# Where five groups of small operations stand in the queues of a projection-bound decoder layer

## The chip, the cores and the metric

The kernel runs on one core of a Trainium2 chip. A core has five engines, each with its own queue that it works through in order: TensorE (PE; its weight loads are listed apart as PEld), VectorE (DVE), ScalarE (ACT), GpSimd (POOL) and SyncE (SP). SP, ACT and POOL also issue DMA transfers from their queues. The time of a kernel is the device time of one execution in microseconds (us); of several runs the median is given.

## The reference

One layer with a residual: a norm, one input projection, three token mixers on separate groups of heads (gated DeltaNet with 6 heads, gated linear attention "GLA" with 5, forgetting attention "fox" with 5), their gates, one output projection, and a final norm. 512 tokens and 16 meta tokens, width 2048, all in float32.

```
h = rms_norm(concat(meta, x), norm_w);  proj = pad(h) @ w_in
qkv = silu(conv4(dq, dk, dv));  q, k = l2_normalize(...)
# gated DeltaNet, chunks of 64, g = cumsum(log_a) in the chunk
decay = exp(where(causal, g[:, None] - g[None, :], -inf))
a_mat = where(strict, (k*beta) @ k.T * decay, 0)
u, w  = triangular_solve(eye + a_mat, [v*beta, k*beta*exp(g)])
# over chunks: v_new = u - w @ s; o = (q*exp(g)) @ s + qk @ v_new; s = s*exp(g_last) + k_dec.T @ v_new
# GLA: chunked linear attention with a decay per key dimension; fox: softmax with cumulative log gates
y = x + concat(dn, gla, fox) @ w_out
return rms_norm(y, final_norm_w)[:, 16:]
```

## The kernel before

**Weights in halves.** The work is bound by two large projections. Float32 precision is kept by splitting each operand in two parts: a high one (rounded to the multiplying type) and a low one (what is left). A "half" is a weight tile `raw` of 128 x 1024 (512 KB), loaded on SP's queue. `split` turns it into `whi` on ACT (line 170) and `wlo` on DVE (line 171); both are recorded with a high priority, and all `wlo` of the program are kept in the list `splits`, all `whi` in `heads_`. PE then makes three products of each 128 x 128 block, high with high, high with low, low with high, so `wlo` is used from the third multiplication of a half on. In the input projection (line 245) a half is 48 multiplications of 264 columns. In the products of the output projection (line 1399, `whia`, `wloa`, `whis`, `wlos`, and at the end `wlh`, `wll`) five pairs of blocks make a product of 60 multiplications of 512 columns.

**Who sets the order.** A scheduler orders the recorded operations on each engine by priority and its own estimate of times. A dependency of kind NoSync between two operations of one engine sets only their order there; one of kind Sync also makes an engine wait for the other. The list `waits` (read at line 1333) takes an operation and a number, and puts the operation behind the split of that number on its engine. `paced` puts an operation behind the newest split on its engine.

**The five places.**

- *Gates and decays.* `gates()` (from line 452) computes the cumulated log decays of 17 heads (6 betas, 6 decays, 5 fox gates in one tile `ga` of 17 rows) on DVE, stores them to DRAM (`gd`, line 467, on ACT's queue), and transposes them to `gcol`. `dn_keys(g)`, for groups g = 0 and 1 of three DeltaNet heads each, loads its rows of `gd` broadcast to all partitions (`gb`, line 657), transposes the keys on PE (`pk`, line 680), and makes the decays: DVE subtracts and clips (line 687: `atm` for the meta tokens, 3 of 16 x 16, and `at`, 12 of 128 x 128), ACT exponentiates (line 688).
- *The inverse.* For each group, the 51 rows of `ab` (48 blocks of 32 x 32, 3 of meta tokens) are inverted row by row on DVE, stored to DRAM (`sc`, line 751), and read back in another layout (`iv`, line 754, and `xm`, line 756), all three on ACT's queue. DVE transposes them (line 760), and PE multiplies on (`pm`, line 766).
- *Sums of x.* For Strassen-like products of the input projection, `x_sums` makes sums of x for eight k, in three calls (0 to 2, 3 to 5, 6 and 7). For each k POOL issues two loads into row buffers (`xa`, `xb`, lines 533 and 534), ACT scales one part (line 537), then come three times a sum on DVE (line 540), its high part `t` on ACT (line 541) and its low part on DVE (line 542).
- *Products of the output projection.* There are seven; behind each, `take` adds the four PSUM banks (`pq`, `pr`, `ps`) to the running outputs `acc`, `accs` on DVE (line 1418).
- *Final weights.* `weigh` multiplies twelve output tiles by the final norm's weights on POOL (line 1428), after their squares have been taken on ACT (line 1425). The last blocks' weights are split at the same time (`wlh`, `wll`).

Of the kernel before, what the change touches and what calls it, by code (L numbers as in the profile page):

```python
# [27 lines left out]
H = 3  # L28
NN = NB * H
# [53 lines left out]
def tile_hybrid_trunk(ctx, tc, xT, xtok, mtok, w_gate, w_in, w_out, w_dn, consts, lmask, fin_w, out, dbg=None):  # L83
# [372 lines left out]
    def gates():  # L456
# [9 lines left out]
        V.tensor_tensor_scan(ga[gr], scm[gr], gt[gr], 0.0, ALU.mult, ALU.add)  # L466
        nc.scalar.dma_start(out=gd, in_=ga[gr])
        pt = psm.tile([P, 512], F32, tag="m", name="ptg")
# [52 lines left out]

    xt_ = {}

    def x_sums(ks):
# [5 lines left out]
        for k in ks:  # L530
            o3 = three[k]
            r1, r2 = row(f"xa{k}")[:, :T], row(f"xb{k}")[:, :T]
            nc.gpsimd.dma_start(out=r1, in_=xT[:, k])
            nc.gpsimd.dma_start(out=r2, in_=xT[:, k + 8])
            x11, x12, x21, x22 = r1[:, :HT], r1[:, HT:], r2[:, :HT], r2[:, HT:]
            w1, w2 = nwc[:, k : k + 1], nwc[:, k + 8 : k + 9]
            A.activation(x11, x11, AF.Copy, scale=w1)
            for i, (n, x, w, less) in enumerate((("t1", x12, w1, x11), ("t2", x22, w2, x12), ("t4", x21, w2, x22))):
                hi, lo = xt_[n, k] = o3[:, i, :HT], o3[:, i, HT:]
                V.scalar_tensor_tensor(out=x, in0=x, scalar=w, in1=less, op0=ALU.mult, op1=ALU.subtract)  # L540
                A.activation(hi, x, AF.Copy, scale=-1.0)
                V.scalar_tensor_tensor(out=lo, in0=x, scalar=-1.0, in1=hi.bitcast(F32), op0=ALU.mult,
                                       op1=ALU.subtract)
# [105 lines left out]
    def dn_keys(g):  # L649
# [25 lines left out]
        for b in (4, 0, 1, 2, 3):  # L675
# [9 lines left out]
            with tc.issue_after(inverse[g - 1]) if g else ExitStack():  # L685
                for j in range(H):
                    V.tensor_scalar(e[:r, j, :], gb[:r, j, ts], gcl(b, j), 0.0, ALU.subtract, ALU.min)
            A.activation(e, e, AF.Exp)
# [37 lines left out]
    def dn_inverse(g, st):  # L726
# [17 lines left out]
        for j in range(1, 31):  # L744
# [4 lines left out]
            V.tensor_tensor(out=a3[:, j + 1 :, 0:j], in0=a3[:, j + 1 :, 0:j], in1=t3, op=ALU.add)  # L749
        sc2 = drp.tile([NN * 4 + H, 1024], F32, tag="sc2", name=f"sc2{g}", bufs=2)  # L750
        nc.scalar.dma_start(out=sc2, in_=ab)
        iv = six.tile([P, 4, NN, 32], F32, tag="six", name=f"iv{g}")
        xc, uc, m1, l1 = (iv[:, i] for i in range(4))
        nc.scalar.dma_start(out=xc, in_=sc2[0 : NN * 4].rearrange("(n r) (a c) -> (r a) n c", r=4, a=32))
        xm = t15(f"xm{g}", (32, H, 32))
        nc.scalar.dma_start(out=xm, in_=sc2[NN * 4 : NN * 4 + H].rearrange("h (a c) -> a h c", a=32))
        um = t15(f"um{g}", (32, H, 32))
# [669 lines left out]
    def weigh(tb, cc):  # L1427
        G.tensor_tensor(out=acc[tb, cc], in0=acc[tb, cc], in1=fw[cc], op=ALU.mult)  # L1428

# [75 lines left out]
    def product(p_, n, weights, first, last):  # L1505
        for j in pairs:
            w = halves(load_s(weights(j), f"{n}{j}"))
            for k in range(4):
                tb, c = k // 2, k % 2
                mms(p_[k], ops[n, j], w[c], slice(tb * P, (tb + 1) * P), first and j == 0, last and j == pairs[-1])  # L1510

    def take(p_, h, J):
        for k in range(4):
            add(2 * h + k // 2, 2 * J + k % 2, p_[k], op=ALU.subtract if J else ALU.add)

# [17 lines left out]
    product(pa, "a22", lambda j: tw[j, 3], False, True)  # L1533
    take(pa, 1, 0)


    fw = []
    for c in range(4):
# [3 lines left out]
    for cc in range(4):  # L1542
# [3 lines left out]
        for kp in kps:  # L1546
            run(pa, cc, kp, kp == kps[0], kp == kps[-1])
            if cc < 3 and (3 == 3 or cc == 2 and kp >= NP // 2 - 3):
                load_last(kp if cc == 2 and 3 < 3 else NP // 2 - 3 + cc)
        if cc == 3:  # L1550
            break
# [3 lines left out]
    for cc in range(3):  # L1555
        for tb in range(4):
            weigh(tb, cc)
    if LAST:
# [97 lines left out]
```

## Time and profile before

| what | us |
|---|---|
| median of three runs | 996.36 |
| lowest, highest | 995.36, 996.70 |
| the profiled execution's own time | 997.14 |
| its span, first to last instruction | 995.4 |
| PE busy | 978.2 |
| DVE busy | 673.5 |
| ACT busy | 480.5 |
| POOL busy | 221.6 |
| mean granted clock of PE | 0.995 |

The trace comes from the profiled execution, so its sums are compared with 997.14 and its span of 995.4. A row of a group or a timeline names the source line, the operation, and what it writes and reads; a bracket gives the idle time of the engine before it and what ended that. A row of the chain gives start and length of a piece of the chain of work that ended last.

### The profile page before, as it was taken

Reading aid. Unit: us, or ns where it says so; the run is one execution under the profiler, and the core shown is the slowest. Engines: PE = TensorE matmul, PEld = TensorE weight load, DVE = VectorE, ACT = ScalarE, POOL = GpSimd, SP = SyncE. Lnnn points to the kernel's source line nnn. Section 1 sums busy time; section 2 is a strip of 40 time slices with the busy share of each in tenths; the row PEclk is TensorE's granted clock in tenths of the full one; section 3 lists DMA queues with packets and bytes.
Section 4 is the critical chain, followed back from the end, with each engine's and each line's share of the span. In section 5 each row is a group of like instructions: output and inputs, shape, how many; then the busy total and the mean of one; then the engine's idle time right before and its main releaser. Section 6 shows DMA issues by size and latency. Waiting matters only on the chain.

```text
span 995.4 us, 19833 instructions
## 1 busy us (share of the span) xinstructions
PE 978.2 (98%) x7762; PEld 895.4 (90%) x7762; DVE 673.5 (68%) x1462; ACT 480.5 (48%) x1051; POOL 221.6 (22%) x237
## 2 busy tenths in 40 slices
PE   9998999999999999999999999999999999999996
PEld 7898999898999988899998988899999998878875
DVE  5456786866666995434684856867768768986674
ACT  7653533324546343424645535655555545644345
POOL 0021222232122334201212221323322120000042
PEclk9999999999999999999999999999999999999998
DMA  9835578977656886645644656678766578356534
GB/s 347 305 107 175 178 220 222 244 216 229 180 164 191 234 237 168 181 105 127 172 117 136 164 142 198 186 215 227 201 198 161 186 268 290 129 208 212 187 111 170
DMA packets 70291, 191.82 MB, mean 193 GB/s; under 512 B 14030, under 2 KB 17278, under 8 KB 69429
## 3 DMA queue, kind: packets, MB, share of 16 engines
q1 hardware_dynamic: 46048, 152.53, 43.9%
q0 software_dynamic: 15104, 31.66, 18.0%
q10 hardware_dynamic: 9044, 6.36, 2.3%
q8 instruction: 61, 1.00, 0.4%
q14 instruction: 34, 0.27, 0.1%
HBM read 179.84 MB, written 60.88 MB: 242 GB/s over the span
## 4 chain that ended last, share of the span: by engine, by line
PE 84%; DVE 7%; DMA 4%; issue 2%; ACT 1%; POOL 1%; ACTq 0%; DVEq 0%; POOLq 0%
PE pp L245 39%; PE pp_a L574 8%; PE pp L314 5%; PE pq L1399 4%; PE pa L1399 3%; PE ps L1399 3%; PE pt L1399 2%; PE pp_b L574 2%; PE pp_d L574 2%; PE pp_c L574 2%; PE pss L1048 1%; DVE wlo L171 1%; PE pgate L431 1%; PE pr L1399 1%; PE pfa L1226 1%
## 5 line engine op out<-in xcount | busy, mean ns | idle before, releaser
L245 PE MATMUL pp<-xh,wlo 128*128 128x264 f32 (+2 forms) x1120 | 274.1, 306 | 3.7 <-DVE wlo L171 3.7
L245 PE MATMUL pp<-xh,whi 128*128 128x264 f32 (+2 forms) x1120 | 273.5, 306 | 0.4 <-ACT whi L170 0.4
L245 PE MATMUL pp<-xl,whi 128*128 128x264 f32 (+2 forms) x1120 | 273.9, 307 | 0.0
L170 ACT CAST whi<-raw 128x1024 fp32r<-128x1024 f32 x131 | 137.2, 1048 | 182.5 <-PE pp L245 94.6
L171 DVE TENSOR_TENSOR wlo<-raw,whi 128x1024 fp32r<-128x1024 f32 x131 | 163.2, 1245 | 69.4 <-ACT whi L170 60.2
L245 PEld LDWEIGHTS pp<-xh,wlo 128*128 128x128 f32 x1120 | 183.6, 189 | 12.9 <-DVE wlo L171 4.4
L245 PEld LDWEIGHTS pp<-xh,whi 128*128 128x128 f32 x1120 | 182.9, 189 | 10.0 <-ACT whi L170 0.6
L245 PEld LDWEIGHTS pp<-xl,whi 128*128 128x128 f32 x1120 | 183.2, 189 | 9.0 <-issue 0.4
L390 POOL TENSOR_SCALAR stc<-cv 128x528 f32<-128x528 f32 (+1 forms) x18 | 28.1, 1563 | 151.0 <-DVE cv L616 148.3
L616 DVE SCALAR_TENSOR_TENSOR cv<-pb,cpk,cv 128x528 f32<-128x528 f32 (+1 forms) x54 | 41.1, 761 | 0.8
L1428 POOL TENSOR_TENSOR acc<-acc,fw 128x512 f32<-128x512 f32 x4 | 6.4, 1619 | 135.7 <-ACT sqf L1425 135.7
L171 DVE TENSOR_TENSOR wlos<-raws,whis 128x1024 fp32r<-128x1024 f32 x20 | 24.1, 1224 | 13.7 <-ACT whis L170 13.6
L170 ACT CAST whis<-raws 128x1024 fp32r<-128x1024 f32 x20 | 20.6, 1050 | 26.0 <-PE pq L1399 11.2
L574 PE MATMUL pp_a<-t,whi 128*128 128x264 f32 (+1 forms) x224 | 30.3, 283 | 0.0
L574 PEld LDWEIGHTS pp_a<-t,whi 128*128 128x128 f32 x224 | 28.0, 188 | 0.4
L574 PE MATMUL pp_a<-xh,whi 128*128 128x264 f32 x112 | 28.1, 285 | 0.0
L574 PE MATMUL pp_a<-xl,whi 128*128 128x264 f32 x112 | 27.9, 285 | 0.0
L1399 PE MATMUL pq<-whia,a 128*128 128x512 f32 x80 | 25.4, 393 | 0.0
L1399 PE MATMUL ps<-whis,s 128*128 128x512 f32 x80 | 25.3, 394 | 0.0
L1399 PE MATMUL pq<-whis,s 128*128 128x512 f32 x80 | 25.3, 394 | 0.0
L390 POOL TENSOR_SCALAR stdz<-zdz 128x512 f32<-128x512 f32 x6 | 11.2, 1876 | 63.1 <-DVE zdz L408 62.1
L493 POOL DMA_DIRECT2D tw<-tw x16 | 13.3, 834 | 45.8 <-DVE wlo L171 31.6
(506 smaller groups left out, 2118.4 us busy)
## 6 DMA issues: line engine op xcount, KB each, us to landing
raw<-in_w_in SPq DMA_DIRECT2D x103, 512.0 KB, 3.8
ti<-in_w_in SPq DMA_DIRECT2D x28, 512.0 KB, 5.4
raw<-ti SPq DMA_DIRECT2D x28, 512.0 KB, 4.0
tw<-in_w_dn SPq DMA_DIRECT2D x20, 512.0 KB, 5.2
raws<-tw SPq DMA_DIRECT2D x15, 512.0 KB, 3.3
ti<-in_w_in POOLq DMA_DIRECT2D x14, 512.0 KB, 5.8
ti<-ti POOLq DMA_DIRECT2D x14, 512.0 KB, 6.3
tw<-in_w_dn POOLq DMA_DIRECT2D x10, 512.0 KB, 6.8
```

Of the source, the lines that this page charges most:

```text
L170: pace[0] = A.copy(hi, raw).ins
L171: pace[1] = V.tensor_tensor(out=lo, in0=raw, in1=hi.bitcast(F32), op=ALU.subtract).ins
L245: mm = PE.matmul(p_[:, :nt], wt[:, j * m : (j + 1) * m], xx[k][:, t0 : t0 + nt], start=(k == 0 and wt is hi and xx is xh), stop=(k == KT - ...
L314: mm = PE.matmul(ps[:, :S], wt[:, j * P : (j + 1) * P], xx[k][:, NM:T], start=(k == 0 and wt is hi and xx is xh), stop=(k == KT - 1 and wt ...
L390: maxes.append(G.tensor_scalar_max(t, src, LOW).ins)
L431: PE.matmul(pgate[a][:, :HT], wg[k // 8][:, k % 8, :], xx[k][:, a * HT : (a + 1) * HT], start=(k == 0 and xx is xh), stop=(k == KT - 1 and ...
L493: x = G.dma_start(out=out_[s], in_=in_[s], accum_op=ALU.add, max_dma_last_dim=2048)
L574: m = PE.matmul(p_[:, cols], wt[:, j * P : (j + 1) * P], xx[j][part_][:, cols], start=first and i == 0, stop=i == len(todo) - 1, skip_grou ...
L616: V.scalar_tensor_tensor(out=c, in0=pb[:, t0 + w : w + T], scalar=cwc[:, blk, w : w + 1], in1=c, op0=ALU.mult, op1=ALU.add)
L1048: mm = PE.matmul(ps[o0 : o0 + n, b * n : b * n + n], kx[rr, k0 : k0 + n], qx[rr, q0 : q0 + n], start=True, stop=True)
L1226: PE.matmul(pa[:, :m], qT[:, ts], kT[:, :m], start=True, stop=True)
L1399: mm = PE.matmul(p_, o_[:, s], w_, start=(first and n == 0), stop=(last and n == 2), skip_group_check=True)
```

## The change

- The store of `gd` is made in two: rows 0 to 15, and row 16. The store of the inverse is made in two: 48 rows to `sc2`, and 3 rows to a DRAM tile `sc3` of their own, from which `xm` is read.
- The decay arguments of group 0 are put behind the newest `wlo` at the time of recording.
- In `x_sums`, for k = 2, 4 and 5, the first scale on ACT and the first sum on DVE are put behind the split that comes one, two and three splits later.
- `take` only notes what is to be added; `flush` makes the additions in the next product, once that has recorded its third weights (j = 2), and puts each behind that split on DVE. The last product's are made directly behind it, as before.
- POOL's final products wait, with a Sync dependency, for the last split of `load_last`: the first three for that of the second call, the nine others for that of the third.

```diff
 def gates():
-        nc.scalar.dma_start(out=gd, in_=ga[gr])
+        nc.scalar.dma_start(out=gd[:16], in_=ga[R0 : R0 + 16])
+        nc.scalar.dma_start(out=gd[16:], in_=ga[R0 + 16 : R1])
...
+    XLATE = {2: 1, 4: 2, 5: 3}
 def x_sums(ks):
-            A.activation(x11, x11, AF.Copy, scale=w1)
+            x = A.activation(x11, x11, AF.Copy, scale=w1)
+            if k in XLATE:
+                waits.append((x.ins, len(heads_) + XLATE[k], heads_))
...
-                V.scalar_tensor_tensor(out=x, in0=x, scalar=w, in1=less, op0=ALU.mult, op1=ALU.subtract)
+                y = V.scalar_tensor_tensor(out=x, in0=x, scalar=w, in1=less, op0=ALU.mult, op1=ALU.subtract)
+                if k in XLATE and i == 0:
+                    waits.append((y.ins, len(splits) + XLATE[k], splits))
...
 def dn_keys(g):
-                    V.tensor_scalar(e[:r, j, :], gb[:r, j, ts], gcl(b, j), 0.0, ALU.subtract, ALU.min)
+                    x = V.tensor_scalar(e[:r, j, :], gb[:r, j, ts], gcl(b, j), 0.0, ALU.subtract, ALU.min)
+                    if g == 0:
+                        tc.add_manual_dep(x.ins, splits[-1].name, mybir.DependencyInfo(
+                            mybir.DependencyClass.NoSync, mybir.DependencyReason.DATA), reason="behind")
...
-        sc2 = drp.tile([NN * 4 + H, 1024], F32, tag="sc2", name=f"sc2{g}", bufs=2)
-        nc.scalar.dma_start(out=sc2, in_=ab)
+        sc2 = drp.tile([NN * 4, 1024], F32, tag="sc2", name=f"sc2{g}", bufs=2)
+        sc3 = drp.tile([H, 1024], F32, tag="sc3", name=f"sc3{g}", bufs=2)
+        nc.scalar.dma_start(out=sc2, in_=ab[: NN * 4])
+        nc.scalar.dma_start(out=sc3, in_=ab[NN * 4 :])
...
     def weigh(tb, cc):
-        G.tensor_tensor(out=acc[tb, cc], in0=acc[tb, cc], in1=fw[cc], op=ALU.mult)
+        return G.tensor_tensor(out=acc[tb, cc], in0=acc[tb, cc], in1=fw[cc], op=ALU.mult)
...
     def product(p_, n, weights, first, last):
         for j in pairs:
             w = halves(load_s(weights(j), f"{n}{j}"))
+            if j == 2:
+                flush()
...
-    def take(p_, h, J):
-        for k in range(4):
-            add(2 * h + k // 2, 2 * J + k % 2, p_[k], op=ALU.subtract if J else ALU.add)
+    taken = []
+
+    def take(*a):
+        taken.append(a)
+
+    def flush():
+        while taken:
+            p_, h, J = taken.pop(0)
+            for k in range(4):
+                paced(add(2 * h + k // 2, 2 * J + k % 2, p_[k], op=ALU.subtract if J else ALU.add))
...
                 load_last(kp if cc == 2 and 3 < 3 else NP // 2 - 3 + cc)
+                marks.append(splits[-1])
...
-            weigh(tb, cc)
+            x = weigh(tb, cc)
+            tc.add_manual_dep(x.ins, marks[1 if cc == 0 and tb < 3 else 2].name, mybir.DependencyInfo(
+                mybir.DependencyClass.Sync, mybir.DependencyReason.DATA), reason="paced")
```

Numbers behind a name count the tiles of the program, and are one to five higher after the change for the same tile; line numbers differ likewise. A row stands for one operation, or for as many as its "x" says.

The decays of group 0 on DVE, before. `wlo_1_1003` is the low half that PE multiplies with next, `wlo_0_1257` that of the half after it, `cv` are the steps of a convolution:

```order
L394 TENSOR_TENSOR kT_683<-cv_802,stc_807 128x528
L379 TENSOR_TENSOR pb_813<-pp_0_815,rstd 128x264
L687 TENSOR_SCALAR atm_1073<-gb_684,gcol 16x16
L379 TENSOR_TENSOR pb_813<-pp_1_816,rstd 128x264
L687 TENSOR_SCALAR atm_1073<-gb_684,gcol 16x16 x2
L687 TENSOR_SCALAR at_1068<-gb_684,gcol 128x128 x10
L171 TENSOR_TENSOR wlo_1_1003<-raw_1_999,whi_1_1002 128x1024
L614 TENSOR_SCALAR cv_929<-pb_813,cpk 128x528
L687 TENSOR_SCALAR at_1068<-gb_684,gcol 128x128 x2
L616 SCALAR_TENSOR_TENSOR cv_929<-pb_813,cpk,cv_929 128x528 x2
L171 TENSOR_TENSOR wlo_0_1257<-raw_0_1253,whi_0_1256 128x1024
```

The same place after:

```order
L394 TENSOR_TENSOR kT_684<-cv_803,stc_808 128x528
L379 TENSOR_TENSOR pb_814<-pp_0_816,rstd 128x264
L379 TENSOR_TENSOR pb_814<-pp_1_817,rstd 128x264
L620 TENSOR_SCALAR cv_930<-pb_814,cpk 128x528
L171 TENSOR_TENSOR wlo_1_1004<-raw_1_1000,whi_1_1003 128x1024
L693 TENSOR_SCALAR atm_1074<-gb_685,gcol 16x16 x3
L693 TENSOR_SCALAR at_1069<-gb_685,gcol 128x128 x3
L622 SCALAR_TENSOR_TENSOR cv_930<-pb_814,cpk,cv_930 128x528
L693 TENSOR_SCALAR at_1069<-gb_685,gcol 128x128 x9
L622 SCALAR_TENSOR_TENSOR cv_930<-pb_814,cpk,cv_930 128x528
L171 TENSOR_TENSOR wlo_0_1258<-raw_0_1254,whi_0_1257 128x1024
```

All fifteen arguments now stand behind the next low half and ahead of the one after it. On PE the transposes of the keys (`pk`) move a half of weights later with them.

The second call of `x_sums` on ACT, before. `gqk` (line 1130) are GLA's normed outputs, which PE transposes next (`pgt`); `t` are high parts of sums of x:

```order
L1126 ACTIVATE gso_5740<-gso_5740,eps_c 128x4
L1127 ACTIVATE gso_5740<-gso_5740 128x4
L541 ACTIVATE t_6739<-xb_6758 128x264
L1130 ACTIVATE gqk_4961<-pgo_5700,gso_5740 128x128 x4
L537 ACTIVATE xa_6771<-xa_6771,cpk 128x264
L541 ACTIVATE t_6739<-xb_6758 128x264
L170 CAST whi_0_7144<-raw_0_7142 128x1024
```

After:

```order
L1137 ACTIVATE gso_5745<-gso_5745,eps_c 128x4
L1138 ACTIVATE gso_5745<-gso_5745 128x4
L1141 ACTIVATE gqk_4966<-pgo_5705,gso_5745 128x128 x4
L170 CAST whi_0_7149<-raw_0_7147 128x1024
L539 ACTIVATE xa_6762<-xa_6762,cpk 128x264
```

The four `gqk` and the weights' high half now stand ahead of the sums of the x for k = 4 (`xa_6762`, with `xb_6763`), and those of k = 5 follow further behind. On POOL the load of the last `xb` of this call moves behind a load of output weights (`tw`) and a memset, and stands right ahead of the select of line 1214.

The additions of the first product (`pq`) on DVE, among the splits of the second product's weights (`wloa`; `ol` are low parts of mixer outputs). Before:

```order
L171 TENSOR_TENSOR wloa_10564<-rawa_10561,whia_10563 128x1024
L627 TENSOR_TENSOR ol_10383<-zfz_9316,oh_10382 128x512
L1418 TENSOR_TENSOR acc_10127<-acc_10127,pq_10441 128x512
L1418 TENSOR_TENSOR accs_10218<-accs_10218,pq_10442 128x512
L1418 TENSOR_TENSOR acc_10129<-acc_10129,pq_10443 128x512
L1418 TENSOR_TENSOR accs_10218<-accs_10218,pq_10444 128x512
L171 TENSOR_TENSOR wloa_10582<-rawa_10579,whia_10581 128x1024
```

After:

```order
L171 TENSOR_TENSOR wloa_10565<-rawa_10562,whia_10564 128x1024
L633 TENSOR_TENSOR ol_10388<-zfz_9321,oh_10387 128x512
L171 TENSOR_TENSOR wloa_10583<-rawa_10580,whia_10582 128x1024
L1429 TENSOR_TENSOR acc_10132<-acc_10132,pq_10446 128x512
L1429 TENSOR_TENSOR accs_10223<-accs_10223,pq_10447 128x512
L1429 TENSOR_TENSOR acc_10134<-acc_10134,pq_10448 128x512
L1429 TENSOR_TENSOR accs_10223<-accs_10223,pq_10449 128x512
```

One more low half has moved ahead of the four additions; the other products change in the same way.

More of the change, by code (lines that the diff above doesn't have):

```diff
@@ L749, in dn_inverse @@
             V.tensor_tensor(out=a3[:, j + 1 :, 0:j], in0=a3[:, j + 1 :, 0:j], in1=t3, op=ALU.add)
-        sc2 = drp.tile([NN * 4 + H, 1024], F32, tag="sc2", name=f"sc2{g}", bufs=2)
-        nc.scalar.dma_start(out=sc2, in_=ab)
+        sc2 = drp.tile([NN * 4, 1024], F32, tag="sc2", name=f"sc2{g}", bufs=2)
+        sc3 = drp.tile([H, 1024], F32, tag="sc3", name=f"sc3{g}", bufs=2)
+        nc.scalar.dma_start(out=sc2, in_=ab[: NN * 4])
+        nc.scalar.dma_start(out=sc3, in_=ab[NN * 4 :])
         iv = six.tile([P, 4, NN, 32], F32, tag="six", name=f"iv{g}")
         xc, uc, m1, l1 = (iv[:, i] for i in range(4))
-        nc.scalar.dma_start(out=xc, in_=sc2[0 : NN * 4].rearrange("(n r) (a c) -> (r a) n c", r=4, a=32))
+        nc.scalar.dma_start(out=xc, in_=sc2.rearrange("(n r) (a c) -> (r a) n c", r=4, a=32))
         xm = t15(f"xm{g}", (32, H, 32))
-        nc.scalar.dma_start(out=xm, in_=sc2[NN * 4 : NN * 4 + H].rearrange("h (a c) -> a h c", a=32))
+        nc.scalar.dma_start(out=xm, in_=sc3.rearrange("h (a c) -> a h c", a=32))
         um = t15(f"um{g}", (32, H, 32))
@@ L1534, in tile_hybrid_trunk @@
     take(pa, 1, 0)
-    fw = []
+    flush()
+    fw, marks = [], []
     for c in range(4):
```

## The prediction

> **What bounds the kernel now.** I read the page's busy shares first, then what TensorE (PE) waited for, then the windows around each of those waits, and last the chain and the timelines of the engines that released them.
>
> ```profile
> PE 978.2 (98%) x7762; PEld 895.4 (90%) x7762; DVE 673.5 (68%) x1462; ACT 480.5 (48%) x1051; POOL 221.6 (22%) x237
> ```
>
> PE is the bound: it is busy 978.2 of the 995.4 us, and no other engine passes 68%. No multiplication is added or removed by this change, so it can only move the 17.2 us in which PE stands still, and the stretches where its clock was low. The waits of PE (columns: sum in us, times, longest):
>
> ```profile
> PE pp L245 <- DVE wlo L171: 3.7, 3, 2.5
> PE pgt L1133 <- ACT gqk L1130: 1.4, 1, 1.4
> PE pr L1399 <- DVE wloa L171: 0.8, 1, 0.8
> PE pt L1399 <- DVE accs L1418: 0.7, 1, 0.7
> PE pm L766 <- DVE iv L760: 0.6, 1, 0.6
> ```
>
> These five make 7.2 us. The rest of the 17.2 lies at the start, behind PE's last instruction and in waits under 0.5, and no part of the change touches the first two. The windows (start and end, length, busy us of PE, its weight loads, DVE, ACT, POOL, then the granted clock, DMA share and GB/s) place the waits in time:
>
> ```profile
> 90.00:92.00 2.00, 1.10 (x10) 0.84 (x8) 2.00 (x12) 1.06 (x3) 0.00 (x0) 1.00 0.00 0
> 92.00:94.00 2.00, 0.36 (x3) 0.36 (x4) 2.00 (x6) 0.75 (x2) 0.00 (x0) 1.00 0.00 0
> 94.00:96.00 2.00, 2.00 (x13) 2.00 (x12) 1.91 (x5) 1.47 (x2) 0.00 (x0) 0.57 0.69 223
> 96.00:98.00 2.00, 2.00 (x12) 2.00 (x12) 1.82 (x2) 0.00 (x0) 0.10 (x1) 0.58 0.80 301
> 222.00:224.00 2.00, 1.51 (x13) 1.30 (x12) 0.81 (x1) 1.39 (x3) 0.00 (x0) 1.00 0.99 152
> 224.00:226.00 2.00, 1.39 (x22) 1.18 (x23) 0.82 (x3) 0.21 (x1) 0.00 (x0) 1.00 1.29 488
> 236.00:238.00 2.00, 1.59 (x13) 1.38 (x12) 1.71 (x5) 1.98 (x4) 0.00 (x0) 1.00 0.87 144
> 238.00:240.00 2.00, 1.31 (x14) 0.97 (x13) 1.89 (x4) 0.60 (x1) 0.00 (x0) 1.00 0.58 104
> ```
>
> PE lost 0.90 + 1.64 = 2.54 us around 92; then two windows stood at a clock of 0.57 and 0.58, in which (0.43 + 0.42) x 2 = 1.70 us of full-speed work were lost. Around 224 and 238 it lost 0.49 + 0.61 + 0.41 + 0.69 = 2.20.
>
> **The change, part by part.**
>
> **Decays.** The chain that ended last, around 80 to 94 (start, us, what):
>
> ```profile
> 77.36 0.78 DVE cv L616
> ...
> 79.43 2.96 DMA gd<-gw
> 82.42 7.15 DMA gb<-gd
> 89.66 0.22 DVE atm L687
> 90.42 2.03 DVE at L687 x10
> 92.45 1.14 DVE wlo L171
> 93.64 3.38 PE pp L245 x16
> ```
>
> VectorE (DVE) works in the order given. The first decay arguments (atm) need the broadcast gb, and the low half of the next weights (wlo) stands behind them, so PE gets it 2.54 us late. The change puts all 15 arguments behind that wlo; in the chain it follows on them without a gap, so DVE alone held it. So this wait goes, and with it the low clock: 2.54 + 1.70 = 4.24. From the other side, the 15 arguments now stand ahead of the following wlo. At 0.20 each (2.03 / 10) they take 3.0 us, and two conv steps (the cv row, 0.78 each) stand among them, 1.6. The rows of PE that set the time for it:
>
> ```profile
> 69.95 1.98 PE pp L245 x16
> ```
>
> ```profile
> 90.50 0.60 PE L680 MATMUL pk<-ident,kT 128*16 128x128 f32 x4
> ```
>
> The first says that 16 multiplications take 1.98 us, so the 48 of a half of weights take 5.9. The second is four transposes of the keys, which the change moves a half on; without them the first half would begin at 90.5, and the following wlo, which the third multiplication of its half uses, is wanted at 90.5 + 5.9 = 96.4. It can be there at 82.42 + 7.15 = 89.57 (gb lands) + 3.0 + 1.6 + 1.14 = 95.3. It fits with about 1 us left, which is thin, so the lower end is 0 gained (the wait comes back a half later); I take the whole, because the store of 16 rows has no more to move than the one of 17. The store of 17 rows as 16 and 1 adds one issue on the queue of ScalarE (ACT), which is 48% busy. What it saves or costs alone lies between -2.96 and +2.96, a store more or less; it is taken at 0, since with the margin of 1 us what waits for gb no longer holds PE.
>
> **Inverse's store.** Chain and timelines around 211 to 226 (in the timelines the bracket is the idle time before, and what ended it):
>
> ```profile
> 211.57 7.10 DMA sc<-ab
> 218.75 6.41 DMA iv<-sc
> 220.51 1.05 ACT L170 CAST whi<-raw 128x1024 fp32r<-128x1024 f32 x1 [9.39 <-DMA raw<-in_w_in]
> 225.18 0.58 DVE L760 STREAM_TRANSPOSE iv<-iv 128x384 f32<-128x384 f32 x1 [2.36 <-DMA iv<-sc]
> ```
>
> The store sc of 51 rows takes 7.10. The loads iv and xm stand on ACT's queue until it has landed, the weights' high half (whi) stands behind them, and DVE's transposes wait for iv. All of the 2.20 us hangs on this chain. 48 rows and 3 rows instead: the nearest small store is gd, 2.96, so the saving lies between 0 (the rows' count does nothing) and 7.10 - 2.96 = 4.1. The two waits that it makes on PE are 0.49 + 0.61 = 1.10 and 0.41 + 0.69 = 1.10, so some 1.5 us saved would do for them; I take all 2.20, lower end 0, which is the price if the load iv or the weights' own arrival holds ACT next. The second issue falls into ACT's 9.39 of idle time. [...]
>
> **Sums of x.** The timelines of DVE and ACT around 545:
>
> ```profile
> 545.44 0.49 DVE L540 SCALAR_TENSOR_TENSOR xb<-xb,cpk,xa 128x264 f32<-128x264 f32 x1 [5.79 <-DMA xb<-in_xT]
> 545.96 0.42 ACT L541 ACTIVATE t<-xb 128x264 fp32r<-128x264 f32 x1 [3.51 <-DVE xb L540]
> 546.29 1.12 ACT L1130 ACTIVATE gqk<-pgo,gso 128x128 f32<-128x128 f32 x4
> ```
>
> gqk was ready, but stood on ACT behind t, which waited for a load of x. The change puts this x's sums behind later weights, so gqk comes first: 1.44 us. Nothing is removed: x's sums, ten operations of 0.4 to 0.5 us for each of three x, run one to three halves later on engines with 32% and 52% of idle time. Between 0 (another operation takes the place) and 1.44, I take 1.44.
>
> **Products' additions.** DVE's timeline, before PE's wait of 0.81:
>
> ```profile
> 871.43 0.70 DVE L1418 TENSOR_TENSOR acc<-acc,pq 128x512 f32<-128x512 f32 x1
> 873.23 0.70 DVE L1418 TENSOR_TENSOR accs<-accs,pq 128x512 f32<-128x512 f32 x1
> 873.82 1.24 DVE L171 TENSOR_TENSOR wloa<-rawa,whia 128x1024 fp32r<-128x1024 f32 x1
> ```
>
> Four additions of 0.6 to 0.7 us run ahead of the third wloa. Behind it, wloa starts 2.4 earlier (873.82 - 871.43), which covers the 0.81 three times: 0.8 gained. The additions then compete with the fourth wloa, and free their bank later. The row under "final weights" below gives 0.224 us per multiplication of this width, so a product of 60 takes 13.4; the bank is wanted a product later, and the additions end at its third half of five, some 5 us ahead. Other products, which wait for nothing now, get the same order; none of their rows tells a wait, so 0, at worst the same 0.8 once again.
>
> **Final weights' products.** Timelines of POOL and DVE, and the chain:
>
> ```profile
> 959.86 4.68 POOL L1428 TENSOR_TENSOR acc<-acc,fw 128x512 f32<-128x512 f32 x3 [0.27 <-ACT sqf L1425]
> 960.14 3.28 DVE L171 TENSOR_TENSOR wll<-rawl,wlh 128x512 fp32r<-128x512 f32 x2
> 967.36 3.05 DVE L171 TENSOR_TENSOR wll<-rawl,wlh 128x512 fp32r<-128x512 f32 x2 [0.43 <-ACT wlh L170]
> 963.34 0.69 DVE accs L1418
> 964.06 21.46 PE pt L1399 x96
> 973.59 5.08 POOL L1428 TENSOR_TENSOR accs<-accs,fw 128x512 f32<-128x512 f32 x4 [2.02 <-ACT sqf L1425]
> ```
>
> Two wll take 3.28, 1.64 each, beside POOL's products, where an operation of the same width (the accs row) takes 0.69. The additions behind them come late and PE waits 0.68. The change lets POOL begin three products behind the second wll pair and nine behind the third, so they no longer meet: 0.7 gained. The third pair starts at 967.36 and takes 1.4 if alone, so POOL goes from 968.8 for 9 x 1.27 (5.08 / 4) = 11.4 us, to 980.2. The last PE row ends at 964.06 + 21.46 = 985.5, and the last block's stores come behind that, so POOL is off the end. Between 0 and 0.7, I take 0.7.
>
> **Sum.** 4.24 + 2.20 + 1.44 + 0.81 + 0.68 = 9.37, against the profiled execution's own 997.14 (span 995.4, 1.74 around it): 987.8. That execution lies 0.78 above the median of 996.36, so 987.0 at the level of the median. Against it I set 0.6, one new wait of the size of the shortest that PE shows above (0.6, for iv): 987.6. About 0.2%, 2.0 us, is what a measurement of this kernel can tell from no change.
>
> **Rivals.**
>
> *Forecast*: every stall goes, with up to 1.5 us of new ones: 986 to 988.6. Chance 0.48.
>
> *One or two of the small places stay.* The store's rows do nothing, say, and 2.20 stays: 987.6 + 2.2 = 989.8; or the sums of x, 989.0. For it: the iv load of 6.41 remains, and the transposes wait for it whatever the store does. Against: only 1.5 of the possible 4.1 us are needed. 988.6 to 990.5. Chance 0.22.
>
> *The low clock stays though the gap goes*: 987.6 + 1.7 = 989.3. The window at 94 shows 0.57 after a gap of 2.54 us, while after the losses around 224 and 238 it stayed at 1.00. The clock may have fallen because of the transposes that ran at 90.50, and not of the gap alone; they still come, a half later. [...] Chance 0.04.
>
> *The decays' wait moves on a half.* If gb lands 1 us later than before, the following wlo or the transposes of the keys, which now come a half later on PE, wait in turn: up to 4.24 back, 991.8. Chance 0.10.
>
> *Slower: POOL's queue.* POOL issues the load of the last x (xb) as soon as the row buffer is free, which the x before it holds, now until its later weights. Behind it on POOL stand a mask on fox scores (L1214), a load of output weights and GLA's factors, for which PE waits.
>
> ```profile
> 559.91 0.29 POOL L1214 TENSOR_SCALAR_AFFINE_SELECT fqk<-fqk 128x128 f32<-128x128 f32 x1 [11.56 <-DMA fqk<-gd]
> ```
>
> POOL has 11.56 us of idle time there, two halves, which covers a delay of two. A delay of four halves leaves two uncovered: PE stands 2 x 5.9, and its clock falls as at 94, 1.7: 987.6 + 11.9 + 1.7 = 1001.2. It decides from 11.56 + 9.4 = 21 us on, since less eats only the gain. For it: three x are moved by one, two and three halves, which add up on one buffer ring. Against: the three lie behind one another anyway. Chance 0.10.
>
> *Within 2 us of before*, where the decays' rival meets two of the small places that stay (991.8 + 2.2 + 0.8 = 994.8): 0.06.
>
> **How the numbers follow.** The likeliest is 987.6, its own range 986 to 988.6. To leave out 2 in 10 the range goes down to 985.6 (the fastest run shown, 995.36, lies 1.0 under the median, and the 0.6 may not come) and up to 992.5 (the decays' rival, with 0.7 more from a second product). Faster by over 0.2%: 0.48 + 0.22 + 0.04 + 0.10 = 0.84; the same 0.06; slower 0.10.
>
> **What would show it.** PE's waits for wlo at 92 and the clock of 0.57 gone; the store of 48 rows under 5.5 us and whi right behind its raw; no wait of pgt for gqk; none of pr for wloa; wll at 0.7 instead of 1.64. Wrong would be: new rows of PE waiting for wlo some 6 us after 92, for kT by the keys' transposes, for POOL's select, or additions holding up a bank.

## The result, and the profile after

The changed kernel takes 986.95 us in the median of six runs (986.75 to 988.19), the kernel before 996.43 on the same chip (995.36 to 997.31): a ratio of 0.9909, 95% interval 0.9896 to 0.9922. The profiled execution took 986.87, with a span of 985.2.

What PE waited for after the change, all of it:

```profile
PE warm L309 <- POOL ones L114: 1.2, 1, 1.2
PE pss L1059 <- issue: 0.5, 1, 0.5
```

The five waits of 7.2 us are gone and none has come in their place; the wait at the start was there before. The windows where the clock had been 0.57:

```profile
90.00:92.00 2.00, 2.00 (x19) 2.00 (x18) 2.00 (x11) 1.26 (x3) 0.00 (x0) 1.00 0.30 127
92.00:94.00 2.00, 2.00 (x18) 2.00 (x18) 2.00 (x4) 1.23 (x3) 0.00 (x0) 1.00 0.00 0
94.00:96.00 2.00, 2.00 (x19) 1.98 (x18) 0.56 (x1) 0.00 (x0) 1.36 (x1) 1.00 0.54 147
96.00:98.00 2.00, 2.00 (x19) 2.00 (x18) 1.44 (x4) 1.79 (x3) 0.22 (x2) 1.00 0.94 377
```

PE is busy throughout at full clock. Where the time went is best read from the moment at which PE reaches the same instruction: up to each of the five moments below PE has begun the same number of instructions before and after, to within one (5754 up to pfa in both). In the view of a tile, each row gives the first and the last start of its instructions. Before:

```profile
L714 PE MATMUL pg<-kT x60: 176/275/276, 121.9 to 336.4; 128*128 128x128 f32 x48, 128*16 128x16 f32 x12
L808 PE MATMUL pu<-m,b x48: 218/218/267, 243.4 to 430.5; 64*64 64x64 f32 x48
L1226 PE MATMUL pfa<-fqk x40: 178/340/503, 660.0 to 842.1; 128*128 128x16 f32 x10, 128*128 128x144 f32 x10, 128*128 128x272 f32 x10, 128*128 128x400 f32 x10
L1399 PE MATMUL ps<-whis,s x80: 387/394/405, 896.5 to 938.0; 128*128 128x512 f32 x80
L1399 PE MATMUL pz<-wlh,oh x6: 222/273/276, 985.4 to 987.0; 128*128 128x128 f32 x6
```

After:

```profile
L723 PE MATMUL pg<-kT x60: 175/275/276, 117.5 to 328.8; 128*128 128x128 f32 x48, 128*16 128x16 f32 x12
L819 PE MATMUL pu<-m,b x48: 217/218/268, 235.9 to 422.9; 64*64 64x64 f32 x48
L1237 PE MATMUL pfa<-fqk x40: 178/340/503, 651.4 to 833.5; 128*128 128x16 f32 x10, 128*128 128x144 f32 x10, 128*128 128x272 f32 x10, 128*128 128x400 f32 x10
L1410 PE MATMUL ps<-whis,s x80: 387/394/404, 886.9 to 928.3; 128*128 128x512 f32 x80
L1410 PE MATMUL pz<-wlh,oh x6: 222/272/277, 974.7 to 976.3; 128*128 128x128 f32 x6
```

| PE reaches (first start) | before | after | earlier by | gained on the way | forecast |
|---|---|---|---|---|---|
| the decays' products (pg) | 121.9 | 117.5 | 4.4 | 4.4 | 4.24 |
| the inverse's last step (pu) | 243.4 | 235.9 | 7.5 | 3.1 | 2.20 |
| the first fox scores (pfa) | 660.0 | 651.4 | 8.6 | 1.1 | 1.44 |
| the fourth product (ps) | 896.5 | 886.9 | 9.6 | 1.0 | 0.81 |
| the last block (pz) | 985.4 | 974.7 | 10.7 | 1.1 | 0.68 |
| the end of the span | 995.4 | 985.2 | 10.2 | -0.5 | 0 |

The last line is a loss: behind PE the end comes half a microsecond later than before. The chain that ended last, after the change, around 965 to 977 (start, us, what):

```profile
964.81 0.70 DVE accs L1429
...
967.97 1.72 DVE accs L1615
969.69 0.61 DVE accs L1429
...
972.48 0.66 DVE accs L1615
973.14 0.61 DVE accs L1429
...
976.60 0.47 DVE accs L1429
```

From 964.81 on the chain runs over DVE and ACT and no longer over PE: each block's sum, its norm and its product with the weights (L1615) follow one another. The first L1615 takes 1.72 in this chain, the second 0.66. POOL's timeline says what ran beside the first:

```profile
958.87 10.27 POOL L1439 TENSOR_TENSOR accs<-accs,fw 128x512 f32<-128x512 f32 x8
```

The products that the change holds back run until 969.14. The stores, on the other hand, are as fast as had been hoped. ACT's queue and DVE around the inverse:

```profile
206.94 0.32 ACTq L761 DMA_DIRECT2D sc<-ab  x1
209.41 0.39 ACTq L765 DMA_DIRECT2D iv<-sc  x1
211.55 1.05 ACT L170 CAST whi<-raw 128x1024 fp32r<-128x1024 f32 x1 [4.80 <-PE pp L245]
214.66 0.58 DVE L771 STREAM_TRANSPOSE iv<-iv 128x384 f32<-128x384 f32 x1 [0.81 <-DMA iv<-sc]
```

The load iv, which waits for the store, is issued 2.5 us behind it, and whi is released by PE and no longer by anything behind the store. The gates' store, in the same queue:

```profile
79.53 0.34 ACTq L467 DMA_DIRECT2D gd<-gw  x1
81.16 0.35 ACTq L663 DMA_DIRECT2D gb<-gd  x1
88.54 0.50 DVE L693 TENSOR_SCALAR atm<-gb,gcol 16x16 f32<-16x16 f32 x3 [1.65 <-DMA gb<-gd]
92.67 1.21 DVE L171 TENSOR_TENSOR wlo<-raw,whi 128x1024 fp32r<-128x1024 f32 x1
```

16 rows land in 1.6 us, where all 17 took 2.96, gb is there 1.1 us earlier (88.54 against 89.66), and the following wlo is done at 93.9, 3 us before PE takes it up at 96.86. (PE's rows of L245 show wlo from the fifth multiplication of a half on, behind two of high with high and two of low with high, and not from the third.)

### The profile page after: what moved, and what is told of

Its sections match the earlier page's. It is cut to its first block, busy times and chain, and to the rows that moved or that the text cites. A ratio compares the mean times of both kernels' runs of the same rounds, so it can differ in the third digit from the quotient of the medians.

```text
span 985.2 us, 19830 instructions
## 1 busy us (share of the span) xinstructions
PE 975.0 (99%) x7762; PEld 894.4 (91%) x7762; DVE 670.5 (68%) x1462; ACT 480.3 (49%) x1051; POOL 218.2 (22%) x237
## 4 chain that ended last, share of the span: by engine, by line
PE 98%; DVE 1%; ACT 1%; issue 0%; POOL 0%; DVEq 0%; ACTq 0%; POOLq 0%
PE pp L245 49%; PE pp_a L580 8%; PE pq L1410 6%; PE pp L314 5%; PE pa L1410 3%; PE ps L1410 3%; PE pt L1410 2%; PE pp_b L580 2%; PE pp_d L580 2%; PE pp_c L580 2%; PE pr L1410 1%; PE pss L1059 1%; PE pgate L431 1%; PE pfo L1285 1%; PE pfa L1237 1%; PE pg L723 1%
## 5 line engine op out<-in xcount | busy, mean ns | idle before, releaser
L245 PE MATMUL pp<-xl,whi 128*128 128x264 f32 (+2 forms) x1120 | 273.9, 306 | 0.0
L245 PE MATMUL pp<-xh,whi 128*128 128x264 f32 (+2 forms) x1120 | 272.9, 306 | 0.0
L245 PE MATMUL pp<-xh,wlo 128*128 128x264 f32 (+2 forms) x1120 | 272.2, 305 | 0.0
L245 PEld LDWEIGHTS pp<-xl,whi 128*128 128x128 f32 x1120 | 182.7, 189 | 9.1 <-issue 0.4
L245 PEld LDWEIGHTS pp<-xh,whi 128*128 128x128 f32 x1120 | 182.3, 189 | 9.2 <-issue 0.2
L245 PEld LDWEIGHTS pp<-xh,wlo 128*128 128x128 f32 x1120 | 182.8, 189 | 8.5 <-issue 0.2
L379 DVE TENSOR_TENSOR pb<-pp,rstd 128x264 f32<-128x264 f32 (+1 forms) x36 | 13.8, 421 | 17.3 <-PE pp L245 17.3
```

The source lines that it names most:

```text
L245: mm = PE.matmul(p_[:, :nt], wt[:, j * m : (j + 1) * m], xx[k][:, t0 : t0 + nt], start=(k == 0 and wt is hi and xx is xh), stop=(k == KT - ...
L379: V.tensor_tensor(out=o, in0=p_[rows], in1=rstd[rows, t0 : t0 + n], op=ALU.mult)
```

## The experiments

They ran on three other chips. On one ran the changed kernel with the decays' order, the inverse's store, the sums of x and the additions undone; on a second the gates' store alone, the store of 34 and 17 rows, POOL's products undone (first run) and one product more; on a third the changed kernel again, POOL's products undone (second run), the decays' order alone, and both. The kernel before takes 994.36, 994.65 and 993.13 us there (medians of 13, 23 and 17 runs), less than the 996.43 above, and varies more: 991.29 to 996.67 over the three. Of these executions no trace was taken; the one trace of the kernel before is that of the first chip. Ratios are to the kernel before on the same chip; differences of an undone part to the changed kernel are read from the traces first, because only the last chip ran that one too.

**The decays' order undone.**

```diff
-                    if g == 0:
+                    if g == 2:
                         tc.add_manual_dep(x.ins, splits[-1].name, ...
```

> The changed kernel with the decay arguments of group 0 not put behind the newest low half, all else as changed. Theory (each stall is a loss of its own): DVE again holds the low half behind gb, which now lands about 1.1 us earlier (88.5), so PE waits some 1.4 us around 91 instead of 2.54; a gap that short leaves the clock at 1.00, so the loss is 1.4 plus a few tenths: 1.4 to 2.0 us, about 988.7. Rival (the transposes of the keys ahead of the gap let the clock fall, not the gap's length): the same wait, but windows at a clock near 0.57 behind it, 3.1 to 3.7 us in all. Second rival (the smaller store had already removed the wait): no change.

988.07 us (986.59 to 990.19), 0.9938 (0.9924 to 0.9952). PE's waits in the profiled execution (987.09):

```profile
PE warm L309 <- POOL ones L114: 1.2, 1, 1.2
PE pp L314 <- ACT xh L302: 0.4, 1, 0.4
PE pss L1059 <- issue: 0.3, 1, 0.3
```

No wait for wlo. The order is that of before, but gb lands early enough:

```profile
87.08 0.23 DVE L693 TENSOR_SCALAR atm<-gb,gcol 16x16 f32<-16x16 f32 x1 [1.99 <-DMA gb<-gd]
87.84 2.04 DVE L693 TENSOR_SCALAR at<-gb,gcol 128x128 f32<-128x128 f32 x10
89.80 1.21 DVE L171 TENSOR_TENSOR wlo<-raw,whi 128x1024 fp32r<-128x1024 f32 x1
```

The second rival held in this execution. wlo is done at 91.0 and PE takes it up at 91.2, with almost nothing to spare, and the broadcast gb, which took 7.3 us in the changed kernel's profile (81.16 to 88.5), took 5.6 here (81.42 to 87.0). Where it takes 7.3 the wait would be back; that the runs spread over 3.6 us fits this, but no profile of this kernel caught one.

**The gates' store alone**, in the kernel before.

```diff
-        nc.scalar.dma_start(out=gd, in_=ga[gr])
+        nc.scalar.dma_start(out=gd[:16], in_=ga[R0 : R0 + 16])
+        nc.scalar.dma_start(out=gd[16:], in_=ga[R0 + 16 : R1])
```

> The kernel before with the gates' store alone made as 16 rows and 1. Theory: gb lands about 1.1 us earlier, PE's wait for the low half at 92 shrinks from 2.54 to about 1.4, and with a gap of that length the clock stays at 1.00: 1.1 + 1.7 = 2.8 us faster, 993.6. Rival (the clock fell because of the transposes ahead of the gap): 1.1 us faster, 995.3, with windows near 0.57.

991.07 us (989.15 to 993.86), 0.9967 (0.9954 to 0.9980): 3.3 us faster, about the theory's 2.8 (the interval is 2.0 to 4.6). Its DVE timeline and PE's waits:

```profile
86.75 0.22 DVE L688 TENSOR_SCALAR atm<-gb,gcol 16x16 f32<-16x16 f32 x1 [1.91 <-DMA gb<-gd]
89.47 1.21 DVE L171 TENSOR_TENSOR wlo<-raw,whi 128x1024 fp32r<-128x1024 f32 x1
```

```profile
PE pgt L1134 <- ACT gqk L1131: 1.6, 1, 1.6
...
PE pr L1400 <- DVE wloa L171: 0.8, 1, 0.8
PE pp L245 <- DVE wlo L171: 0.7, 1, 0.7
...
PE pt L1400 <- DVE accs L1419: 0.3, 1, 0.3
```

In the windows PE is busy from 86 to 98 without a break, at a clock of 1.00; the waits for wlo and whi lie later, at the inverse. Neither the theory's rest of 1.4 nor the rival's low clock is there, so this run does not tell what sets the clock: gap and low clock went together. (In the profile before, the gap of 1.44 around 545 left the clock at 1.00 in the windows from 544 to 548.) Nor is the early gb the work of the smaller store by itself: of the 2.9 us by which it comes earlier than in the profile before (86.75 against 89.66), 1.2 lie at the moment of its issue (81.19 against 82.42) and the rest in its own time, 5.5 us instead of 7.15. In eleven traces the rows show gb, from its issue to the first of the decay arguments: 7.0 to 7.4 us in five and 5.6 to 5.9 in six. Both traces with the whole store are among the five, and so are three with the store in two; whether the store in two also makes gb faster stays open.

**The decays' order alone, and both**, in the kernel before.

```diff
+                    if g == 0:
+                        tc.add_manual_dep(x.ins, splits[-1].name, ... "behind")
```

> The kernel before with the decay arguments alone put behind the next low half, its gates' store whole. Theory (either of the two, the smaller store or the order, removes the wait at 92, since the store alone gave 3.3 us): 3.3 to 4.5 us faster than the kernel before, no wait of PE near 92 and a clock of 1.00. Rival (the order only moves the wait to the next low half, because gb lands as late as before): 0 to 2 us faster, PE waits for wlo near 97.

991.49 us (989.88 to 992.87), 0.9978 (0.9966 to 0.9989): 2.2 us faster. It was less than expected, but on a chip where the kernel before takes less (993.13). The mechanism is the theory's, since in spite of the whole store the following wlo comes in time:

```profile
89.61 0.50 DVE L687 TENSOR_SCALAR atm<-gb,gcol 16x16 f32<-16x16 f32 x3 [2.15 <-DMA gb<-gd]
93.74 1.21 DVE L171 TENSOR_TENSOR wlo<-raw,whi 128x1024 fp32r<-128x1024 f32 x1
```

gb lands at 89.6, as late as before, wlo is done at 95.0, PE takes it up at 96.95, and waits nowhere between 90 and 98. With the store in two beside it:

> The kernel before with the gates' store in two and the decay arguments behind the next low half. Theory (the two remove the same wait): the same as the better of the two alone within 1 us, 3.5 to 4.5 us faster than the kernel before. Rival (each has a gain of its own): their sum, 6 us or more.

991.51 us (989.48 to 993.41), 0.9973 (0.9960 to 0.9987): 2.7 us (1.3 to 4.0), the same as one alone within the intervals, and less than the 5.5 of the two together. The two parts remove one and the same wait. Their gains do not add up.

**The inverse's store made whole again.**

```diff
-        nc.scalar.dma_start(out=sc2, in_=ab[: NN * 4])
-        nc.scalar.dma_start(out=sc3, in_=ab[NN * 4 :])
+        nc.scalar.dma_start(out=sc2, in_=ab)
```

> The changed kernel with the inverse's store made whole again (51 rows), read by both loads as before. Theory: the store lands in about 7.1 us instead of 2.5, ACT's high half stands behind it, PE's waits around 222 and 236 come back: idle 2.20 plus the restarts, 3.0 to 3.3 us by the moments at which PE reached the same instructions (5.8 against 4.4 us apart at the first, 7.5 behind the second); about 990.1. Rival (the other parts had moved ACT's order so that the store no longer holds the weights): 0 to 1 us.

989.20 us (987.62 to 993.29), 0.9956 (0.9940 to 0.9972). The wait is back, but smaller in the profiled execution (988.04), and the time spreads over 5.7 us from run to run. The chain, and PE's wait:

```profile
207.13 5.73 DMA sc<-ab
```

```profile
PE pp L245 <- DVE wlo L171: 0.6, 1, 0.6
```

The whole store took 5.73 here, against 7.10 in the profile of before. How much it costs goes with this time. From pg to pu PE takes 118.4 us in the changed kernel; with the whole store it takes 119.2 to 120.0 in the three traces where the store took 5.7 to 5.8 (this run, and the gates' store and the decays' order alone), and 121.4 and 121.5 in the two where it took 7.1 to 7.2 (both together, and the kernel before). So the same store costs 0.8 to 1.6 us in one case and 3.0 to 3.1 in the other.

**The store as 34 and 17 rows.**

```diff
-        nc.scalar.dma_start(out=sc2, in_=ab[: NN * 4])
-        nc.scalar.dma_start(out=sc3, in_=ab[NN * 4 :])
+        nc.scalar.dma_start(out=sc2[:34], in_=ab[:34])
+        nc.scalar.dma_start(out=sc2[34:], in_=ab[34:])
...
```

(This is the changed kernel; both pieces go into one DRAM tile of 51 rows, and `xm` is read from it.)

> The changed kernel with the inverse's store made in two pieces of 34 and 17 rows, into one DRAM tile. [...] Rival (two smaller stores are faster because each has less to move): landing in about 4.7 us, no wait or 1 us at most.

994.88 us (992.64 to 997.68), 1.0007 (0.9993 to 1.0021): as slow as the kernel before, so this store costs as much as all the rest of the change brings. The chain and PE's waits:

```profile
207.44 9.21 DMA sc<-ab
...
382.69 12.62 DMA sc<-ab
```

```profile
PE pp L245 <- ACT whi L170: 3.6, 2, 2.0
PE pp L245 <- DVE wlo L171: 1.6, 3, 0.5
```

The second row of the chain is the second group's store. It holds PE too (1.97 and 0.51 us at 398), at a place where no other trace has a wait: there the whole store of the kernel before, 8.9 us from its issue to that of the load behind it, came in time.

The rival (smaller stores are faster) falls: two pieces, with the same bytes as the one of 51 rows, land 9.5 us behind the first issue at 207.15, where 51 rows took 5.7 to 7.2 and 48 and 3 rows took 2.5 in the changed kernel. The rival had 4.7. Why these three differ in this way was not shown: how a transfer is spread over the DMA engines is in no row.

**The sums of x, undone.**

```diff
-    XLATE = {2: 1, 4: 2, 5: 3}
+    XLATE = {}
```

> The changed kernel without the three x being put behind later splits. Theory: PE's wait for gqk of 1.4 us is back, 1.1 to 1.5 us, about 988.2; nothing elsewhere. Rival (the load of x arrives at another time now that all before it runs 7.5 us earlier, so the wait was an accident of one schedule): less than 0.4 us.

987.55 us (987.32 to 990.38), 0.9939 (0.9925 to 0.9953). The wait is back in its place:

```profile
PE pgt L1144 <- ACT gqk L1141: 1.2, 1, 1.2
```

It is not an accident of one schedule: 1.4, 1.6 and 1.2 us in three kernels with different starts, and 1.8 in two more without this part (the decays' order alone, and both).

**The products' additions, undone.**

```diff
             w = halves(load_s(weights(j), f"{n}{j}"))
-            if j == 2:
-                flush()
...
     def take(*a):
         taken.append(a)
+        flush_now()
```

(and the additions without `paced`.)

> The changed kernel with the products' additions made directly behind their product again. Theory: PE waits for one wloa, 0.8 idle and 1.0 with the restart, about 987.9. Rival (the new order of the other products had given gains or losses of its own, which cancel): anything from -0.5 to 0.5 us.

988.50 us (988.03 to 989.52), 0.9942 (0.9930 to 0.9954). One wait, the old one, and no other:

```profile
PE pr L1410 <- DVE wloa L171: 0.8, 1, 0.8
```

**POOL's final products, undone**, twice; the second time beside the changed kernel.

```diff
-            x = weigh(tb, cc)
-            tc.add_manual_dep(x.ins, marks[1 if cc == 0 and tb < 3 else 2].name, ... "paced")
+            weigh(tb, cc)
```

> The changed kernel without the dependency that holds POOL's final products back. Theory: the splits of the last weights take 1.6 us each beside POOL again and PE waits about 0.7 around 953, which costs 1.0 at PE's end; but PE's end no longer sets the end of the kernel alone: the tail behind PE, 8.4 us in the changed kernel against 7.95 before, falls back to 7.95. Net 0.5 to 0.7 us slower, about 987.5. Rival (the longer tail has nothing to do with POOL): the full 1.0 slower, with a tail of 8.4.

987.76 us (985.89 to 989.25), 0.9932 (0.9917 to 0.9948), with a span of 984.2 in the profiled execution, 1.0 shorter than the changed kernel's. The theory was wrong in its first half: wll takes 1.2 to 1.5 us beside POOL again (two in 2.38, two in 2.96), but PE does not wait. By the times it is no faster than the changed kernel elsewhere (ratios 0.9932 here, 0.9935 in the next run).

> The changed kernel as it is, on the chip of the three runs beside it, since chips differ by some us. Theory: 0.7 to 0.9% faster than the kernel before on this chip too. Its tail behind PE's last multiplication is 0.4 to 0.8 longer than that of the kernel before and of the one beside it without the hold on POOL.

987.21 us (986.95 to 987.78), 0.9935 (0.9923 to 0.9947): 0.65% faster, a little less than expected.

> The changed kernel without the hold on POOL's final products, a second time, now beside the changed kernel. The first run's profile showed PE ending at the same moment as in the changed kernel (976.4 and 976.5) and a shorter tail. Theory (the hold gives PE nothing here and costs the tail, since a DVE product of two SBUF inputs meets POOL): 0.3 to 0.9 us faster than the changed kernel. Rival (PE's wait of 0.7 for the additions comes back in most executions, the first profile was a lucky one): 0.2 to 0.7 slower.

986.17 us (985.83 to 987.79), 0.9929 (0.9915 to 0.9943). The medians lie 1.0 us apart in favour of the kernel without the hold; the intervals of the two ratios overlap, so the order is likely and not proven by the times. The traces show the place. The changed kernel on this chip, its DVE and the end of its chain:

```profile
968.94 1.78 DVE L1615 SCALAR_TENSOR_TENSOR accs<-accs,frs,fw 128x512 f32<-128x512 f32 x1
973.43 0.74 DVE L1615 SCALAR_TENSOR_TENSOR accs<-accs,frs,fw 128x512 f32<-128x512 f32 x1
980.66 0.71 ACT accs L1613
```

Without the hold, DVE, POOL and the chain's end:

```profile
967.99 0.74 DVE L1613 SCALAR_TENSOR_TENSOR accs<-accs,frs,fw 128x512 f32<-128x512 f32 x1
962.72 5.07 POOL L1439 TENSOR_TENSOR accs<-accs,fw 128x512 f32<-128x512 f32 x4 [1.41 <-ACT sqf L1436]
978.72 0.71 ACT accs L1611
```

POOL is through at 967.8, the first L1613 takes 0.74 instead of 1.78, and the chain ends 1.9 us earlier: about 1.0 because PE ends earlier (its last multiplication starts at 976.3 against 977.3; the changed kernel had one more wait of 0.5 elsewhere, and PE is as far behind at ps, 887.7 against 886.7, where no product of POOL has begun), and 0.9 behind PE. This kernel, the change without its last part, has the lowest median of all that were run, in this second run; in its first, on another chip, it had 987.76.

**One product more ahead of the hold.**

```diff
-marks[1 if cc == 0 and tb < 3 else 2]
+marks[1 if cc == 0 else 2]
```

> The changed kernel with four, not three, of POOL's products released by the second call's split and eight by the third's. Theory: POOL ends 1.3 us earlier, about 967.8, so DVE's product of two SBUF inputs at 967.9 takes 0.75 instead of 1.79 and the chain of the last blocks on DVE and ACT, which sets the end, is 0.4 shorter: 986.5. Rival: the fourth product meets the third pair of splits at 956.3, which then take 1.6 each, and PE waits 0.5 or more: 987.0 to 987.6.

987.18 us (986.83 to 991.05), 0.9934 (0.9917 to 0.9950): the same as the changed kernel on the last chip (0.9935). The profiled execution was the slowest (991.05), with waits of 1.4, 1.3 and 0.8 us in places that the edit does not touch. In it the first L1615 starts at 973.12, after POOL's last product has ended at 972.91, and takes 0.74, as the theory says; no wait of PE stands near the third pair of splits. But the instruction ahead of it on DVE now meets POOL in its place:

```profile
971.81 1.39 DVE L1617 TENSOR_SCALAR accs<-accs,frs 128x512 f32<-128x512 f32 x1 [0.58 <-ACT frs L1609]
```

It takes 1.39 here, and 0.48 for the block behind it, when POOL has ended. The delay has moved by one instruction, and the times do not show a gain.

## Why the prediction was right, and where not

The forecast of 987.6 is 0.6 over the measured 986.95, and within its own range of 986 to 988.6. The likeliest case came about: every stall went. But the sum came out through errors that cancel, and it fits the chip whose trace it was read from: on the last chip the same change brings 6.5 us (a ratio of 0.9935) where the sum says 9.37.

- *Decays, 4.24.* PE gained 4.4 there, and the low clock went with the gap. Beside the order, taking the gates' store at 0 was right in the sum: both together gain no more than one. But the step "saves or costs alone" weighed only its landing, up to 2.96, and not that an earlier gb can take the whole wait away without the order: alone it gives 3.3 us. And 4.24 is the loss of one execution with a late gb; in the runs the order alone gives 2.2, so this term was too large for the other chips. The order is likely the safer cure, since it held with a gb as late as before (89.6), while the store only makes gb earlier; the store alone with a gb of 7 us was not caught in a trace.
- *Inverse's store, 2.20.* Undersized for this profile: 3.1 by the moments at which PE reached pu. The estimate that 1.5 us saved at the store would remove the waits did not hold either: with a store of 5.7 to 5.8 us, 1.3 to 1.4 shorter, 0.8 to 1.6 us of the loss remain. The bounds for the landing were 2.96 to 7.10, and it came in 2.5, below the row of gd; gd's 17 rows were themselves slow (2.96, against 1.6 for its 16) and so no fair floor.
- *Sums of x, 1.44, and products, 0.81.* 1.1 and 1.0 by the moments, and the waits come back as 1.2 and 0.8 when undone. With the sums of x undone PE takes 416.6 us from pu to pfa; in the changed kernel, and with the decays' order, the additions or the hold undone, it takes 415.1 to 416.0. So this order is worth 0.6 to 1.5, which holds both the 1.1 and the forecast's 1.44.
- *Final weights, 0.68.* Wrong. The step that failed is "POOL is off the end". It was argued from the last block's stores, and overlooked that DVE multiplies the first block's last tile (L1615) while POOL still works. DVE's instruction then takes 1.7 to 1.8 instead of 0.74, and the chain behind it is a chain of DVE and ACT. Nor is the 1.1 of the table's last block the hold's work: from ps to pz PE takes 87.8 us in the changed kernel, 87.8 in both profiles without the hold and 87.8 in the kernel before with the gates' store and the decays' order alone, against 88.9 in the profile before. Two profiles without the hold show no wait of PE for the additions either, and two kernels built on the one before (the decays' order, and both) none, a third 0.3. So the wait of 0.68 goes without the hold too. In these profiles the part costs more than it brings; the times make that likely.
- *0.6 for a new wait.* None came in this profile (one of 0.5 in the second profile of the changed kernel). It stood against gains that were too small by about as much, which is luck.
- *Rivals.* The decays' wait did not move on: wlo was done at 93.9, not 95.3, because gb came earlier, and with a late gb (the order alone) at 95.0, still 2 us ahead of PE. POOL's queue delayed nothing that PE waits for. The low clock left with the gap, which agrees with the forecast: in the changed kernel's trace every window of 2 us from 4 to 974 us has a clock of 1.00, and so has every window from 86 to 98 in five other runs (the decays' order undone, the inverse's store whole, one product more, the gates' store alone, 34 and 17 rows); in each of the six the same four transposes run there, 0.60 us between 90.6 and 97.3. The profiled execution of the kernel before has a mean clock of 0.995, the thirteen others 0.997 or 0.998. The longest wait of PE in them, 1.97 us, is in the run with 34 and 17 rows, whose mean is 0.998, at 398, where no such transposes run (in the changed kernel's trace their last start is at 314.5); what length of gap, with or without them, lowers the clock was not tried.

The five terms of the forecast give 9.37 us (7.67 of idle time and 1.70 of low clock), the moments give 10.7. The rest of 1.3 stands in rows counted as busy: PE's busy time fell by 3.2 (978.2 to 975.0), of which the clock explains 1.7. What the other 1.5 are was not settled; the first multiplication of 512 columns behind a wait is listed with 0.50 us (at 875.12 before, behind the 0.81 for wloa) where the others have 0.39 or 0.40.

## What to carry to other kernels

A wait that rests on a small DMA store through DRAM can be removed at the store (here 48 and 16 rows, with the few others in a store of their own) or at the queue (what the weights wait for goes first); try one alone before counting both. Where the kernel before spreads by 5 us from run to run, a loss read from one of its executions is the loss of that execution. When all of the bound engine's waits went here, the end passed to the engines behind it (DVE and ACT, from 964.81 on), so whatever is moved late must be checked against every operation of that tail, and not against the last one alone. In these two places a store more was worth it: 48 and 3 rows landed in 2.5 us where 51 took 5.7 to 7.2, and 16 rows in 1.6 where 17 took 2.96. Two pieces of 34 and 17 rows, with 9.5, were worse than one of 51.

## What the runs showed of the hardware that was not expected

- The same DMA differs between traces: the first group's whole store of 51 rows took 5.7 to 5.8 us in three and 7.1 to 7.2 in two, the broadcast of gb 5.6 to 5.9 in six and 7.0 to 7.4 in five. An estimate from the rows above says what this does to the kernel before: with a gb of 5.5 instead of 7.15 the gap of 2.54 at the decays would be 0.9, and if it left the clock up, 3.3 of the 4.24 would go; with a store of 5.7 another 1.5 to 2.3, by the moments from pg to pu. That is 4.8 to 5.6 us, as much as the kernel's spread; no trace of a faster execution of it shows this. The kernel before, with waits behind both, spread over 5.4 us on the last chip (991.29 to 996.67 in 17 runs), the changed kernel beside it over 0.8 (986.95 to 987.78 in 6). The gain differs with the chip: 0.91% on the first, 0.65% on the last.
- The granted clock over a whole execution of the kernel before lay between 0.993 and 0.998 on the second chip, with 996.16 us at 0.993 and 991.90 at 0.998; but another execution at 0.998 took 995.91, so the clock does not set the time alone. The run with the gates' store alone had 0.996 to 0.998 there.
- A DVE product of two SBUF inputs (L1615) beside POOL's products took 1.78 and 1.79 us in the two traces of the changed kernel, and 0.74 to 0.75 once POOL had ended. The DVE product ahead of it, of one wide SBUF input and one factor for each partition (L1617), took 0.70 to 1.39 us beside POOL instead of 0.49.
